# Two tile sizes that move SBUF addresses, and a new order for the first feed-forward step, in a two-layer hybrid decoder

## The chip, the cores and the metric

The kernel runs on one core of one Trainium2 chip. Time is the device time of one execution in microseconds. The span that a profile covers is shorter than that execution's own time by a little over 2 us here. Three runs of the kernel before lie within 0.1% of each other.

The engines are named as in the profile: PE is the TensorE matmul, PEld its load of the stationary operand, DVE VectorE, ACT ScalarE, POOL GpSimd, SP SyncE (here it issues the DMAs).

## The reference

A trunk of two layers on a sequence of 1024 rows of width 1024, in float32. Layer 0 mixes tokens with a gated linear recurrence, layer 1 with stick-breaking attention of 16 heads. Each mixer is followed by a feed-forward block of inner width 2816, and at the end there is a normalization.

```python
for layer in range(DEPTH):                      # DEPTH = 2
    hn = rms_norm(h, mix_norm[layer])
    mixed = rg_lru_block(hn, ...) if layer % 2 == 0 else stick_breaking_attention(hn, ...)
    h = h + mixed
    h = h + swiglu_ffn(rms_norm(h, ffn_norm[layer]), ffn_w_in[layer], ffn_w_out[layer])
return rms_norm(h, final_norm)

def swiglu_ffn(x, w_in, w_out):
    gu = x @ w_in
    return (silu(gu[..., :D_FF]) * gu[..., D_FF:]) @ w_out
```

## The kernel before

**Numbers.** Every float32 matmul is made of three in a reduced format (float32r): operand = high part + low part, and the product is high·high + low·high + high·low. The helper `mm3` (lines 639, 640 and 641) issues the three, each with 128x128 stationary and 128x512 moving operand, so almost every PE instruction of the page is one of these lines. ACT makes the high part (a copy that rounds), DVE the low part (a subtraction).

**Stages in time.** The recurrence and its projections run from 0 to about 321 us (the last 384 matmuls of it are its output projection), feed-forward 0 from there to about 965 us, attention to about 1470, attention's output projection to 1536, feed-forward 1 to the end.

**Feed-forward.** Both matrix products use Strassen-like schemes: a 2x2 block product is made from seven products (numbers 0 to 6, done in the order 0, 1, 2, 3, 4, 6, 5, `ORDER`). For the input side the seven combinations of the activations lie in SBUF once, as tiles `v[i, j]` (high `vh`, low `vl`; i is the product, j one of four blocks of the contraction). For each of the 22 column blocks f there is a *step* of 7 x 4 x 3 = 84 matmuls against seven combinations of that block's weights: `wa` serves products 0 and 1, `wb` 2 and 4, `wc` 3 and 5, `wd` 6 (with h or l for the part). The weights of a step are prepared during the step ahead of it by `a_hi`, `a_lo`, `s12`, `s2`, `s3`, `b_hi`, `do_s4`, and in the step itself by `b_lo`, `c_hi`, `c_lo`, `d_hi`, `d_lo` (lines 1116 to 1161). `post` takes a product out of its PSUM bank (lines 1302 to 1315), `gate` multiplies by the normalization factor and applies SiLU (1320 to 1326), and `operands` stores the result for the output side (1334 to 1350). The output side then runs 13 *visits* of the same seven products over 2 to 4 blocks each. Products that share a bank within a step (0, 2, 4, 5 in the first, 3 and 6 in the third, table `BANK`) accumulate on each other, so the next may start only when `post` has copied what was there.

**The first step.** The column block f = 0 is done ahead of the loop, all seven products at once in an order of its own (`P0`): first the blocks j = 0, 1, 2 of six products (54 matmuls), then j = 3 of the six and product 6. The first pass of the loop (`s_ == 0`, f = 1) also finishes the sums of squares of the normalization (`squares`), sums them over the partitions with PE (`Factors.sums`, line 597) and makes the factors (`all_factors`: two square roots and two squares on ACT, lines 600 and 603, four operations on DVE, lines 606 and 609), gates f = 0 and prepares f = 2. Its order is what the loop's body says. The order of the other engines in the loop is written out by hand too, as the body is emitted; in the recurrence and the attention a planner (`Plan`) sets it from estimated durations.

**Where tiles lie.** Pools are stacks. One grows from the low end of a partition's bytes: constants (`cp`), three raw weight buffers (`rp`), the activations `xh`/`xl` (`xp`), and later, in the place of these, part of the tiles `v` (`vp0`: all with i = 6, all with j = 3, and (5, 2)), the gate buffers, and the attention's pool `ap`. The other grows from the high end (`side="right"`): the ring of prepared weights (`wp`, `wq`), h, and the other tiles `v` (`vp1`). The last tile of `cp` is `minus` with 144 columns, of which only column 0 is used. In `ap` the tile `vt` holds 1024 columns and a margin of 32.

By the addresses of the build, the weight ring begins at byte 212864 of a partition and `vp1` at 85888; both leave 128 when divided by 256, and the tiles in them are multiples of 512 bytes. `minus` begins at 6592 and has 576 bytes, so `rp` begins at 7168 and `xp` and `vp0` at 19456, which leave 0. In `ap`, the two `vt` tiles (4224 bytes each) put about half of the tiles at 0 and half at 128.

Of the kernel before, what the change touches and what calls it, by code (L numbers as in the profile page):

```python
# [504 lines left out]
def trunk(  # L505
# [67 lines left out]
            for d in range(ND):  # L573
                x_[d] = [xp.tile([P, NB], F32R, name=f"{nm}{d}_{n}") for n in range(NH)]
    rcol = cp.tile([P, NT], F32, name="rcol")
    minus = cp.tile([P, 144], F32R, name="minus")
    fresh = tiny[:, 60:61]
    nc.gpsimd.memset(fresh, -(2.0**-41))
    nc.vector.tensor_copy(minus[:, 0:1], fresh)
# [31 lines left out]
    def all_factors(sums):  # L611
        for step in ("root", "square", "newton", "out"):
            for t in sums:
                getattr(t, step)()
# [444 lines left out]
    def mix_out_ffn_in(h, mix, bias, layer, gnext, ob):  # L1059
# [132 lines left out]
        with tc.manual_schedule(engines={E.PE, E.Activation, E.DVE, E.Pool}):  # L1192
# [505 lines left out]
            def seam(w):  # L1698
# [53 lines left out]
                pre["at"] = {k: end[t] - free["pe"] for k, t in marks.items()}  # L1752
                pre["raw"] = raws

            last_use = {p: max(u for u, (_, p0, p1) in enumerate(VISITS) if p0 <= p < p1) for p in range(NF // 2)}
            for s_, (kind, x) in enumerate(steps[:looped]):
                w, nw, ahead = nw, nxt, None
                if s_ + 2 < len(steps) - final:
                    ahead = weights_of(*steps[s_ + 2])

                g = {5: (0, 1), 6: (2, 3)} if s_ == 0 else {0: (1,), 1: (2,), 2: (3,)}
                gf = x - 1 if kind == "f" else NF - 1 if x == 2 else None
                if gf is not None and s_:
                    gate(gf, 0)
                if not w.ready:
                    w.b_lo()
                    if kind == "f":
                        w.c_hi()
                banks = {}
                if kind == "f":  # L1770
                    rhs = rhs_in
                else:
                    _, p0, p1 = VISITS[x]
                    rhs = {i: [R[p][i] for p in range(p0, p1)] for i in range(NPROD)}
                for k, i in enumerate(ORDER):
                    b = BANK[i]
                    new = b not in banks
                    if new:
                        banks[b] = pp.tile([P, NB], F32, tag="p", name=f"p{i}_ps")
                    if s_ == 0 and k == 4:  # L1780
                        part(banks[b], w, i, rhs[i], range(1), onto=not new)
                        for t in sums:
                            t.sums()
                        part(banks[b], w, i, rhs[i], range(1, HK), onto=not new)
                        UT.append(big("U", 2))
                        ta, tb = (pair_tile(x) for x in ("ta", "tb"))
                        nw.a_lo()
                        nw.s2()
                        nw.s3()
                        all_factors(sums)  # L1790
                    else:
                        part(banks[b], w, i, rhs[i], range(len(rhs[i])), onto=not new)
                    if kind == "f":
                        post(x, i, banks[b])
                    else:
                        old = done[:]
                        del done[:]
                        post_out(x, i, banks[b])
                        for dn in old:
                            if s_ == looped - 1 and k >= L - 2:  # L1800
                                done.append(dn)
                            else:
                                finished(*dn)
                    if s_ == 0:
                        if k < 2:
                            for _ in range(2):
                                squares(h, *sq_todo.pop(0), rbc, acc, V)

                    if k == 0:
                        if kind == "v":  # L1810
                            w.c_hi()
                        w.c_lo()
                    elif k == 2:
                        w.d_hi()
                        w.d_lo()
                        if nw:
                            nw.a_hi()
                        if s_ == 0:
                            for t in sums:
                                t.hi()  # L1820
                                t.lo()
                    elif nw:
                        if k == 3:
                            nw.s12()
                        elif k == 4 and s_:
                            nw.a_lo()
                            nw.s2()
                            nw.s3()
                        elif k == 5:
                            nw.b_hi()  # L1830
                            nw.do_s4()
                    if ahead and k == 3:
                        ahead.load_a()
                    elif ahead and k == 5:
                        ahead.load_b()

                    if gf is not None:
                        for y in g.get(k, ()):
                            gate(gf, y)
                        if gf % 2 == 0:  # L1840
                            if k == L - 1 and gf < NF - 2:
                                operands(gf // 2, 0)
                        elif 3 <= k <= 5:
                            if gf == NF - 1 and k == 3:
                                operands(gf // 2, 0)
                            operands(gf // 2, k - 2)

                    if kind == "f":
                        split_ahead(x - 7, k)
                    if kind == "f" and x == NF - 1:  # L1850
                        for p, y, _ in PLACES[k]:
                            if p < 2:
                                bring(p, y)
                        for y in {5: (0, 1, 2, 3, 4), 6: (6, 5)}.get(k, ()):
                            bring(2, y)
                    if kind == "v" and x == 0 and k == 5:
                        for y in ORDER:
                            bring(3, y)
                    if kind == "v":
                        gone = [p for p in range(NF // 2 - 4) if last_use[p] == x]  # L1860
                        for y, p in enumerate(gone):
                            bring(p + 4, i)
                            tasks.append((L * (x + 1) + k + 2 + y, p + 4, i))
                        if final and x == NV - 3 and k == 0:
                            for y in range(2):
                                bring(NF // 2 - 2 + y, 7, C[3][ORDER[y]])
                                tasks.append((L * (x + 1) + 3 + y, NF // 2 - 2 + y, 7))
                            d, p0, p1 = VISITS[NV - 1]
                            for y in range(2):
                                src = ffn_w_out[layer, d + y * HK][:, :, p0 * P : p1 * P]  # L1870
                                nc.sync.dma_start(held[5 + y].rearrange("p (y c) -> p y c", y=2), src)
                            nc.sync.dma_start(
                                held[3].rearrange("p (x c) -> p x c", x=2)[:, :, 0:P],
                                fin.broadcast_to([P, 2 * P]).rearrange("p (x c) -> p x c", x=2),
                            )
                            nc.scalar.sqrt(tiny[:, 62:63], ones)
                    if (kind == "v" and k < L - 1) or (kind == "f" and x == NF - 1):
                        now = k + (0 if kind == "f" else L * (x + 1))
                        tasks.sort(key=lambda t: t[0])
                        while tasks and tasks[0][0] <= now:  # L1880
                            split_op(*tasks.pop(0)[1:])
                nxt = ahead
                if kind == "v" and final:
                    if x == 2:
                        open_end()
                elif kind == "v":
                    if x == 2:
                        open_first()
                    elif x == NV - 3:
                        open_last()  # L1890
# [29 lines left out]
    with ExitStack() as st:  # L1920
# [51 lines left out]
        def scaled(q, which, n):  # L1972
            ps = PS.pop((q, which, n))
            if which < 2:
                t = TT[n] = own([P, NB], f"t{n}")
            else:
                if n == 0:
                    VT[q] = own([P, S + 32], f"vt{q % 2}")
                    nc.gpsimd.memset(VT[q][:, 15:16], 0.0)
                t = VT[q][:, 16 + n * NB : 16 + (n + 1) * NB]  # L1980
            V.tensor_mul(t, ps, rbc[n])
# [263 lines left out]
```

## Time and profile before

| | |
|---|---|
| median of 3 runs | 2198.35 us (2197.18 to 2198.82) |
| the profiled execution's own time | 2198.75 us |
| its span in the profile | 2196.5 us |
| PE, PEld busy | 2180.4 us (99%), 1782.3 us (81%) |
| DVE, ACT busy | 1714.3 us (78%), 1098.0 us (50%) |
| DMA | 274.61 MB, mean 125 GB/s |
| granted TensorE clock | 0.999 |

A PE row's duration (some 393 ns for 512 columns) is the time from the first column read to the last result and overlaps the next row's; what a matmul costs in a stream is the distance from its start to the start of the next. The rows of a timeline give starts to 0.01 us, so such a distance is best taken over many rows.

### The profile page before, as it was taken

What the parts mean: (1) busy time and instruction counts of PE and PEld (TensorE: products, weight loads), DVE (VectorE), ACT (ScalarE), POOL (GpSimd) and SP (SyncE); (2) the same over time, 40 slices, a digit from 0 to 9 for tenths busy, and PEclk for the clock granted to TensorE, in tenths of its full rate; (3) what the DMA queues carried; (4) which work ended last, traced back from release to release, by engine and by line L of the source; (5) the groups of instructions that cost most, each with busy time, mean ns of one, the idle gap of its engine ahead of it and who ended that gap; (6) DMA issues with size and microseconds to landing.
All of it is one profiled execution on the core that took longest, in us unless ns stands there. A gap on an engine that the chain in (4) does not pass through costs nothing.

```text
span 2196.5 us, 27019 instructions
## 1 busy us (share of the span) xinstructions
PE 2180.4 (99%) x9954; PEld 1782.3 (81%) x9954; DVE 1714.3 (78%) x2416; ACT 1098.0 (50%) x1793; POOL 29.3 (1%) x40
## 2 busy tenths in 40 slices
PE   9999999999999999999999999999999999999998
PEld 7888887888888888878888888888788888888887
DVE  8878678667777887888888888867866766777877
ACT  6577445344343544565555555544534434454555
POOL 0000020000000000000000000002000000000000
PEclk9999999999999999999999999999999999999999
DMA  4111312344443764444333333631133444467452
GB/s 174 39 48 48 119 45 68 105 129 145 144 149 128 258 213 125 141 135 113 92 101 93 100 92 101 186 143 65 58 115 117 144 143 143 140 224 245 129 160 84
DMA packets 133316, 274.61 MB, mean 125 GB/s; under 512 B 15296, under 2 KB 23872, under 8 KB 133184
## 3 DMA queue, kind: packets, MB, share of 16 engines
q1 hardware_dynamic: 132768, 272.36, 39.0%
q8 instruction: 78, 1.28, 0.2%
q10 hardware_dynamic: 416, 0.52, 0.1%
q14 instruction: 54, 0.44, 0.1%
HBM read 176.88 MB, written 70.78 MB: 113 GB/s over the span
## 4 chain that ended last, share of the span: by engine, by line
PE 97%; DVE 2%; ACT 1%; issue 0%; DMA 0%; DVEq 0%; ACTq 0%
PE p_ps L639 19%; PE p_ps L641 19%; PE p_ps L640 19%; PE qk_ps L639 4%; PE qk_ps L641 4%; PE qk_ps L640 4%; PE z_ps L2044 3%; PE av_ps L2092 3%; PE wt_ps L2075 3%; PE a_ps L640 3%; PE a_ps L641 3%; PE a_ps L639 3%; PE ob_ps L639 2%; PE ob_ps L640 2%; PE ob_ps L641 2%; PE g_ps L641 1%
## 5 line engine op out<-in xcount | busy, mean ns | idle before, releaser
L639 PE MATMUL p_ps<-vh,wbh 128*128 128x512 f32 x524 | 206.6, 394 | 3.3 <-ACT G L1302 2.2
L641 PE MATMUL p_ps<-vh,wbl 128*128 128x512 f32 x524 | 206.2, 394 | 3.2 <-DVE wbl L1142 3.2
L639 PE MATMUL p_ps<-vh,wch 128*128 128x512 f32 x524 | 206.1, 393 | 0.0
L641 PE MATMUL p_ps<-vh,wal 128*128 128x512 f32 x524 | 205.6, 392 | 0.2 <-DVE wal L1133 0.2
L640 PE MATMUL p_ps<-vl,wbh 128*128 128x512 f32 x524 | 205.8, 393 | 0.0
L640 PE MATMUL p_ps<-vl,wch 128*128 128x512 f32 x524 | 205.6, 392 | 0.0
L639 PE MATMUL p_ps<-vh,wah 128*128 128x512 f32 x524 | 205.6, 392 | 0.0
L641 PE MATMUL p_ps<-vh,wcl 128*128 128x512 f32 x524 | 205.4, 392 | 0.0
L640 PE MATMUL p_ps<-vl,wah 128*128 128x512 f32 x524 | 205.0, 391 | 0.0
L1138 ACT CAST wbh<-sb 128x1024 fp32r<-128x1024 f32 (+2 forms) x69 | 69.7, 1010 | 193.1 <-DVE sb L1122 193.1
L2056 ACT ACTIVATE F<-z_ps 128x512 f32<-128x512 f32 (+3 forms) x188 | 92.1, 490 | 98.3 <-PE z_ps L2044 97.1
L2080 ACT CAST th<-wt_ps 128x512 fp32r<-128x512 f32 x192 | 92.2, 481 | 85.1 <-PE wt_ps L2075 77.3
L2063 DVE TENSOR_TENSOR_SCAN F<-F,unit 128x128 f32<-128x128 f32 (+3 forms) x128 | 104.7, 820 | 33.6 <-ACT F L2056 32.5
L641 PEld LDWEIGHTS p_ps<-vh,wbl 128*128 128x128 f32 x524 | 98.6, 188 | 26.7 <-DVE wbl L1142 4.0
L639 PEld LDWEIGHTS p_ps<-vh,wbh 128*128 128x128 f32 x524 | 98.6, 188 | 26.4 <-ACT G L1302 3.0
L2084 DVE TENSOR_TENSOR tl<-wt_ps,th 128x512 fp32r<-128x512 f32 x192 | 104.6, 545 | 16.8 <-ACT th L2080 16.7
L641 PEld LDWEIGHTS p_ps<-vh,wal 128*128 128x128 f32 x524 | 98.3, 188 | 23.3 <-DVE wal L1133 1.3
L641 PEld LDWEIGHTS p_ps<-vh,wcl 128*128 128x128 f32 x524 | 98.3, 188 | 22.9 <-DVE wcl L1152 0.3
L640 PEld LDWEIGHTS p_ps<-vl,wch 128*128 128x128 f32 x524 | 98.5, 188 | 22.5
L640 PEld LDWEIGHTS p_ps<-vl,wbh 128*128 128x128 f32 x524 | 98.6, 188 | 22.2
L639 PEld LDWEIGHTS p_ps<-vh,wch 128*128 128x128 f32 x524 | 98.5, 188 | 22.2
L639 PEld LDWEIGHTS p_ps<-vh,wah 128*128 128x128 f32 x524 | 98.4, 188 | 22.2
(436 smaller groups left out, 5499.8 us busy)
## 6 DMA issues: line engine op xcount, KB each, us to landing
raw<-in_ffn_w_in SPq DMA_DIRECT2D x88, 512.0 KB, 3.6
vl<-pd SPq DMA_DIRECT2D x128, 256.0 KB, 3.4
pd<-U SPq DMA_DIRECT2D x90, 256.0 KB, 2.2
raw<-in_ffn_w_out SPq DMA_DIRECT2D x28, 512.0 KB, 4.0
raw<-in_attn_w_qkv SPq DMA_DIRECT2D x24, 512.0 KB, 3.8
kh<-qh SPq DMA_DIRECT2D x64, 128.0 KB, 2.3
kl<-ql SPq DMA_DIRECT2D x64, 128.0 KB, 2.3
acc<-pd SPq DMA_DIRECT2D x28, 256.0 KB, 2.6
```

The lines of the kernel that those rows point to most:

```text
L639: nc.tensor.matmul(ps, lhsT=wh, rhs=mh, start=first, stop=False, **kw)
L640: nc.tensor.matmul(ps, lhsT=wh, rhs=ml, start=False, stop=False, **kw)
L641: nc.tensor.matmul(ps, lhsT=wl, rhs=mh, start=False, stop=last, **kw)
L1138: nc.scalar.copy(self.full(self.wb), self.full(self.sb))
L2044: nc.tensor.matmul(ps[:, 0:n], lhsT=lhsT, rhs=rhs, start=i == 0, stop=i == 1)
L2056: nc.scalar.activation(F, Z.pop(c)[:, 0:n], AF.Sigmoid, scale=-SC)
L2063: V.tensor_tensor_scan(rev, rev, unit[:, NB - n :][:, ::-1], 0.0, op0=ALU.mult, op1=ALU.add)
L2075: nc.tensor.transpose(tp[:, c : c + P], F[:, (kb % 4) * P : (kb % 4 + 1) * P], ident)
L2080: nc.scalar.copy(WH[u][:, c:], TP[u][:, c:])
L2084: V.tensor_sub(WL[u][:, c:], TP.pop(u)[:, c:], f32(WH[u])[:, c:])
L2092: nc.tensor.matmul(ps[:, c:], lhsT=VV[q][:, kb, hx], rhs=t.pop(u)[:, c:], start=kb == 4 * G and i == 0, stop=kb == 3 and i == 1,)
```

## The change

Two tile sizes: `minus` shrinks from 144 to 112 columns (576 to 448 bytes), and `vt` grows from 1024 + 32 to 1024 + 64 columns (4224 to 4352 bytes). By the addresses of the new build, everything in the low stack behind `minus` moves down by 128 bytes: `rp` now begins at 7040, `xp` and `vp0` at 19328, and all 792 tiles of `ap` leave 128 when divided by 256. The high stack stays where it was. One pool that leaves 128 before leaves 0 now: `sp`, with the first four weight columns of the recurrence (`fh`, `fl`).

An order: in the first pass of each layer's loop, from product 2 on (k = 2 to 6), the body is replaced by a function `opening` that says what ACT, DVE and SP do after each product. It has the same instructions in another order; the `b_lo` of f = 2 is moved out of the second pass into the end of the first. PE's and SP's order is unchanged.

```diff
-    minus = cp.tile([P, 144], F32R, name="minus")
+    minus = cp.tile([P, 112], F32R, name="minus")
...
+            def opening(k, banks, w, nw, ahead):
+                ps = banks[BANK[ORDER[k]]]
+                if k == 2:
+                    post(1, 2, ps)
+                    for step in ("hi", "lo"):
+                        for t in sums:
+                            getattr(t, step)()
+                    w.d_hi()
+                    w.d_lo()
+                elif k == 3:
+                    nw.s12()
+                    nw.s2()
+                    nw.s3()
+                    ahead.load_a()
+                elif k == 4:
+                    all_factors(sums)
+                    post(1, 3, banks[BANK[3]])
+                    nw.a_hi()
+                    nw.a_lo()
+                    gate(0, 0)
+                    post(1, 4, ps)
+                    nw.b_hi()
+                elif k == 5:
+                    gate(0, 1)
+                    post(1, 6, ps)
+                    nw.do_s4()
+                    ahead.load_b()
+                else:
+                    post(1, 5, ps)
+                    nw.b_lo()
+                    gate(0, 2)
+                    gate(0, 3)
+                    operands(0, 0)
...
-                g = {5: (0, 1), 6: (2, 3)} if s_ == 0 else {0: (1,), 1: (2,), 2: (3,)}
+                g = {0: (1,), 1: (2,), 2: (3,)} if s_ else {}
...
                 if not w.ready:
-                    w.b_lo()
+                    if s_ != 1:
+                        w.b_lo()
                     if kind == "f":
                         w.c_hi()
...
-                        nw.a_lo()
-                        nw.s2()
-                        nw.s3()
-                        all_factors(sums)
                     else:
                         part(banks[b], w, i, rhs[i], range(len(rhs[i])), onto=not new)
+                    if s_ == 0 and k > 1:
+                        opening(k, banks, w, nw, ahead)
+                        continue
...
-                        if s_ == 0:
-                            for t in sums:
-                                t.hi()
-                                t.lo()
...
-                    VT[q] = own([P, S + 32], f"vt{q % 2}")
+                    VT[q] = own([P, S + 64], f"vt{q % 2}")
```

The order on ACT around the factors, in layer 0 (`U_2760` and `ta` hold the high parts of the sums of squares, `U_2548` is a gate buffer of f = 1, `p_ps` a product's bank, `wah` the weights of f = 2). Before:

```order
L1158 CAST wd<-s_2742 128x512
L1129 CAST wah<-raw 128x1024
L590 CAST U_2760<-acc_1874 128x512
L590 CAST ta<-acc_1875 128x512
L1308 COPY U_2548<-p_ps 128x512
L600 ACT_TABLE_LOAD
L600 ACTIVATE acc_1874<-ob,tiny 128x512
L600 ACTIVATE acc_1875<-ob,tiny 128x512
L603 ACTIVATE rbc_83<-acc_1874 128x512
L603 ACTIVATE rbc_84<-acc_1875 128x512
L1310 COPY U_2548<-p_ps 128x512
```

And now:

```order
L590 CAST U_2760<-acc_1874 128x512
L590 CAST ta<-acc_1875 128x512
L1158 CAST wd<-s_2742 128x512
L600 ACT_TABLE_LOAD
L600 ACTIVATE acc_1874<-ob,tiny 128x512
L600 ACTIVATE acc_1875<-ob,tiny 128x512
L603 ACTIVATE rbc_83<-acc_1874 128x512
L603 ACTIVATE rbc_84<-acc_1875 128x512
L1308 COPY U_2548<-p_ps 128x512
L1129 CAST wah<-raw 128x1024
L1310 COPY U_2548<-p_ps 128x512
```

The casts for the sums of squares come earlier, the copy of product 3 (L1308) now stands behind the four factor operations, and the weights `wah` stand behind it.

The order on DVE from the factors to the start of the second pass (`G_2545` and `U_2547` are f = 0's gate buffers, `G_2546` is f = 1's; `wbl` is f = 2's low part). Before:

```order
L609 SCALAR_TENSOR_TENSOR ob<-rbc_84,acc_1875 128x512
L1311 TENSOR_TENSOR U_2548<-U_2548 128x512
L1313 TENSOR_TENSOR G_2546<-G_2546,p_ps 128x512
L1125 TENSOR_TENSOR s_2868<-sb,raw 128x512
L1320 TENSOR_TENSOR G_2545<-ob,G_2545 128x1024
L1324 TENSOR_TENSOR G_2545<-ob,G_2545 128x1024
L1326 TENSOR_TENSOR U_2547<-U_2547,G_2545 128x1024
L1336 TENSOR_TENSOR ta<-U_2547 128x512
L1320 TENSOR_TENSOR G_2546<-ob,G_2546 128x1024
L1142 TENSOR_TENSOR wbl<-sb,wbh 128x1024
```

And now:

```order
L609 SCALAR_TENSOR_TENSOR ob<-rbc_84,acc_1875 128x512
L1133 TENSOR_TENSOR wal<-raw,wah 128x1024
L1320 TENSOR_TENSOR G_2545<-ob,G_2545 128x1024
L1311 TENSOR_TENSOR U_2548<-U_2548 128x512
L1313 TENSOR_TENSOR G_2546<-G_2546,p_ps 128x512
L1125 TENSOR_TENSOR s_2865<-sb,raw 128x512
L1142 TENSOR_TENSOR wbl<-sb,wbh 128x1024
L1324 TENSOR_TENSOR G_2545<-ob,G_2545 128x1024
L1326 TENSOR_TENSOR U_2547<-U_2547,G_2545 128x1024
L1336 TENSOR_TENSOR ta<-U_2547 128x512
L1320 TENSOR_TENSOR G_2546<-ob,G_2546 128x1024
```

The low part `wbl` (L1142) moves ahead of f = 0's second and third gate operations and of f = 1's first; `wal` (L1133) moves from before the factors to behind them. Layer 1 has the same two changes.

More of the change, by code (lines that the diff above doesn't have):

```diff
@@ L1804, in mix_out_ffn_in @@
                     if s_ == 0:
-                        if k < 2:
-                            for _ in range(2):
-                                squares(h, *sq_todo.pop(0), rbc, acc, V)
+                        for _ in range(2):
+                            squares(h, *sq_todo.pop(0), rbc, acc, V)
                     if k == 0:
@@ L1824, in mix_out_ffn_in @@
                             nw.s12()
-                        elif k == 4 and s_:
+                        elif k == 4:
                             nw.a_lo()
```

## The prediction

> **What bounds the kernel now.** I read the page's busy shares and the chain of waits first, then PE's waits, then PE's timeline, since the first two leave only one engine.
>
> ```profile
> PE 2180.4 (99%) x9954; PEld 1782.3 (81%) x9954; DVE 1714.3 (78%) x2416; ACT 1098.0 (50%) x1793; POOL 29.3 (1%) x40
> PE 97%; DVE 2%; ACT 1%; issue 0%; DMA 0%; DVEq 0%; ACTq 0%
> PE p_ps L641 <- DVE wbl L1142: 3.2, 2, 1.6
> PE p_ps L639 <- ACT G L1302: 2.2, 2, 1.1
> PE a_ps L774 <- POOL ident masks.py:199: 1.5, 1, 1.5
> PE p_ps L639 <- ACT ta L1738: 1.2, 1, 1.2
> ```
>
> The last four rows are PE's longest waits of the whole execution: total, times, longest. Two of the four are the two layers' openings, 5.4 us together. Nothing else is on the path but the stream of matmuls itself. So the question is how fast that stream runs, and whether it runs equally fast everywhere. It doesn't:
>
> ```profile
> 322.87 0.39 PE L639 MATMUL p_ps<-vh,wah 128*128 128x512 f32 x1
> ...
> 332.39 0.40 PE L639 MATMUL p_ps<-vh,wch 128*128 128x512 f32 x1
> ...
> 340.08 0.39 PE L639 MATMUL p_ps<-vh,wah 128*128 128x512 f32 x1
> ```
>
> This is the column block done ahead of the loop in layer 0. From 320.81 to 332.39 PE runs 51 matmuls whose `v` tiles lie in the high stack (blocks 0 to 2 of six products, without (5, 2)); all operands leave 128 modulo 256. From its tenth on (322.87) these are 42 in 9.52 us, 226.7 ns each. From 332.39 to 340.08 come 33 whose `v` tiles lie in the low stack and leave 0, against weights that leave 128: 7.69 us, 233.0 ns each. Same instruction, same weights' ring, no wait in either, 6.3 ns apart.
>
> Now the same distance where the kernel spends its time:
>
> ```profile
> 52.01 0.40 PE L639 MATMUL a_ps<-xh,whi 128*128 128x512 f32 x1
> ...
> 320.81 0.39 PE L639 MATMUL p_ps<-vh,wah 128*128 128x512 f32 x1
> 480.11 0.39 PE L639 MATMUL p_ps<-vh,wah 128*128 128x512 f32 x1
> ...
> 499.47 0.39 PE L639 MATMUL p_ps<-vh,wah 128*128 128x512 f32 x1
> 978.63 0.39 PE L639 MATMUL qk_ps<-xg,whi 128*128 128x512 f32 x1
> ...
> 993.96 0.23 PE L2044 MATMUL z_ps<-kh,q 128*128 128x128 f32 x1
> 1469.55 0.39 PE L639 MATMUL ob_ps<-vh,whi 128*128 128x512 f32 x1
> ...
> 1536.47 0.39 PE L639 MATMUL p_ps<-vh,wah 128*128 128x512 f32 x1
> ```
>
> Recurrence and its output projection: 1152 matmuls from 52.01 to 320.81, all with moving operands in the low stack, 268.80 / 1152 = 233.3 ns. One feed-forward step: 84 in 19.36 us = 230.5 ns; 33 of its 84 read low-stack tiles. Attention's projections where nothing is between them: 66 in 15.33 us = 232.3 ns. Attention's output projection in layer 1: 288 in 66.92 us = 232.4 ns. Every stretch falls between the two values of the pair above, the feed-forward step, where most addresses agree, lowest.
>
> **The change part by part.** *Addresses.* The new sizes put both operands at 128 modulo 256 everywhere but in the first 192 matmuls. I take 226.7 ns for each matmul of 512 columns and subtract:
> - recurrence: 1152 x (233.3 - 226.7) = 7.6 us;
> - feed-forward: 22 steps x 84 + 44 blocks x 21 = 2772 in a layer, 5544 in all, x (230.5 - 226.7) = 21.1 us;
> - output projection of layer 1: 288 x (232.4 - 226.7) = 1.6 us;
> - attention: 1152 projection matmuls x (232.3 - 226.7) = 6.4 us. The products z and av have 384 more of 512 columns, mixed with 128-wide ones; no row there is a clean pair, so they are worth 0 to 2.2 us.
>
> What hides behind PE must keep up:
>
> ```profile
> 50.00:308.00 258.00, 258.00 (x1108) 207.51 (x1107) 198.13 (x232) 148.26 (x170) 9.07 (x7) 1.00 0.19 60
> 400.00:900.00 500.00, 500.00 (x2171) 407.01 (x2170) 372.36 (x519) 219.03 (x346) 0.00 (x0) 1.00 0.48 158
> 980.00:1477.00 497.00, 496.15 (x2633) 414.92 (x2632) 418.03 (x619) 270.72 (x539) 0.59 (x6) 1.00 0.39 111
> ```
>
> After the length come PE, PEld, DVE, ACT. DVE is busy 77%, 74% and 84% of these stretches, so a PE that is 1.6 to 2.8% faster doesn't reach it on average. In the attention the chain z, sigmoid, scan, transpose, av goes round all engines with two banks each, and local waits can eat a part; its bounds are 0 (DVE paces it) and 8.6 us, and I take 5.5, nearer the upper, because PE waits nowhere in its main part. Sum of the addresses: 7.6 + 21.1 + 1.6 + 5.5 = 35.8 us.
>
> *The openings.* Layer 0, second pass, product 2:
>
> ```profile
> 365.96 0.40 PE L641 MATMUL p_ps<-vh,wal 128*128 128x512 f32 x1
> 367.44 0.50 PE L639 MATMUL p_ps<-vh,wbh 128*128 128x512 f32 x1 [1.08 <-ACT G L1302]
> 367.78 0.39 PE L640 MATMUL p_ps<-vl,wbh 128*128 128x512 f32 x1
> 369.76 0.50 PE L641 MATMUL p_ps<-vh,wbl 128*128 128x512 f32 x1 [1.59 <-DVE wbl L1142]
> 360.46 0.39 PE L641 MATMUL p_ps<-vh,wcl 128*128 128x512 f32 x1
> 365.49 1.23 DVE L1326 TENSOR_TENSOR U<-U,G 128x1024 f32<-128x1024 f32 x1
> 366.80 0.59 ACT L1302 COPY G<-p_ps 128x512 f32<-128x512 f32 x1 [1.09 <-DVE U L1326]
> 368.49 1.22 DVE L1142 TENSOR_TENSOR wbl<-sb,wbh 128x1024 fp32r<-128x1024 f32 x1
> ```
>
> Starts that should be 0.23 us apart are 1.48 and 1.98 apart: 1.25 + 1.75 = 3.0 us lost a layer. Cause: the copy L1302 of product 0 into f = 0's buffer waits for the last gate operation (L1326) on that buffer, and `wbl` stands behind it on DVE. Now `wbl` comes first. Its ring buffer is `wch` of the pass before, free when that pass's last product ends (360.46 in the old order), so it runs from about 361.5 to 362.7; L1324 and L1326 follow, 1.23 us each, to 365.2; the copy ends near 365.9. PE wants bank and weights at 366.7, later by the new stall below. Both waits go, with under a microsecond to spare.
>
> Something is late in their place: product 6 accumulates onto product 3's bank, and the copy L1308 of that bank now stands behind the factors.
>
> ```profile
> 348.32 0.39 PE L641 MATMUL p_ps<-vh,wbl 128*128 128x512 f32 x1
> 348.75 0.59 ACT L1306 COPY G<-p_ps 128x512 f32<-128x512 f32 x1 [0.83 <-PE p_ps L641]
> 352.72 0.48 PE L597 MATMUL ob<-tb,minus 128*128 128x512 f32 x1
> 353.64 1.27 ACT L600 ACTIVATE acc<-ob,tiny 128x512 f32<-128x512 f32 x2
> 354.80 1.16 ACT L603 ACTIVATE rbc<-acc 128x512 f32<-128x512 f32 x2
> 355.85 0.58 ACT L1310 COPY U<-p_ps 128x512 f32<-128x512 f32 x1
> 355.12 0.39 PE L639 MATMUL p_ps<-vh,wd 128*128 128x512 f32 x1
> ```
>
> ACT follows a PE result 0.43 us after that matmul's start (348.32 to 348.75). The square roots need the sums, last started at 352.72, so they begin near 353.15 instead of 353.64 (the table load before them is earlier by the copy that left, and no longer the last to finish). L603 comes 1.16 later, L1308 another 1.05 later, at 355.36, and ends 0.59 later at 355.95. Product 6 would start at 355.12. New stall: about 0.9 us a layer; bounds 0.4 (if the square roots take the first sum as soon as it is there) and 1.2. Net 3.0 - 0.9 = 2.1 a layer, 4.2 us.
>
> *The clock.* In layer 1 the same two stalls end in a stretch at a lower clock:
>
> ```profile
> 1586.00:1590.00 4.00, 4.00 (x12) 3.13 (x11) 2.30 (x3) 0.58 (x2) 0.00 (x0) 0.57 0.43 131
> ```
>
> The granted clock was 0.57 in these 4 us, 4 x 0.43 = 1.7 us lost; layer 0, with equal stalls, has no such stretch. With one stall of 0.9 us in place of two within 4 us I take the 1.7 back. [...]
>
> *Nothing else.* The order of PE and SP is the same, so no transfer is issued earlier or later by the order; `vt`'s extra columns aren't touched.
>
> Sum: 35.8 + 4.2 + 1.7 = 41.7 us from the profiled execution's 2198.75 gives 2157.0; the median lies 0.4 below that execution, so 2156.7. I say **2157 us**.
>
> **The rivals.** *Other engines pace the attention and the output visits.* For it: DVE's 84%. Against it: no PE wait in the attention's main part. Then 5.5 us and 44 x 21 x 2 x 3.8 ns = 7.0 us stay: about 2169.5.
>
> *The addresses are not the cause.* The pair differs also in which block is done; were it the tile's place in the scheme, only the openings would count: 2198.35 - 5.9 = 2192.5. Against it: the recurrence has no scheme, all its moving tiles in the low stack, and 233.3 ns.
>
> [...]
>
> *Slower: agreement is what costs.* Operands at the same place in a 256-byte line could collide at every read, and the weight load become the bound.
>
> ```profile
> L639 PEld LDWEIGHTS p_ps<-vh,wbh 128*128 128x128 f32 x524 | 98.6, 188 | 26.4 <-ACT G L1302 3.0 <-ACT ta L1738 1.6
> ```
>
> A load takes 188 ns and fits under a matmul with some 40 to spare. If it grew past 233, each nanosecond over would cost 8.1 us on the 8,136 matmuls named above (mean now 231.2); at 237 ns it would be 2198 + 47 - 6 = 2239. It decides from 232 ns on, where the openings' 5.9 us are used up. Against it: 51 matmuls in agreement at 320.81 to 332.39 show the opposite.
>
> *The change doesn't do what it says*: a pool's start could be rounded up again. The build's addresses speak against that; 2192.5 again.
>
> **How the numbers follow.** Forecast 72%, other engines pace 16%, addresses not the cause or not moved 7%, agreement costs 3%, the rest 2%. The forecast's own bounds: attention 0 to 8.6 us, openings' stall 0.4 to 1.2 in two layers, the clock 0 to 1.7, and small new waits of about 2 us: 2152 to 2167. For 8 in 10 I reach to the second case and a little past both: 2148 to 2171. Less than 0.2% (4.4 us) can't be told from no change here. Faster 95%, same 2%, slower 3%.
>
> **What would show it.** In the recurrence the 1152 matmuls should take 261.2 us (226.7 each), a step of feed-forward 19.04 us, the projections of the attention 15.0 us for 66. If they stay at 233.3, 230.5 and 232.3, the addresses fall. PE's list of waits should lose `wbl` and L1302 and gain the copy L1308 at two times about 0.9 us, and the clock row of layer 1 should read 1.00. If the attention stays at its length while its PE gains waits on DVE, the second case holds. I am wrong above 2171 or below 2148.

## The result, and the profile after

The changed kernel takes **2163.56 us** (median of 4 runs, 2163.40 to 2163.97); the kernel before takes 2198.41 beside it. The ratio is 0.9843, with a 95% interval of 0.9826 to 0.986: 34.9 us less, where 41.7 were forecast. The profiled execution took 2163.40 us with a span of 2161.1.

First the page's shares, busy time by engine and the chain that ended last.

```profile
PE 2148.0 (99%) x9954; PEld 1781.1 (82%) x9954; DVE 1716.3 (79%) x2416; ACT 1098.5 (51%) x1793; POOL 29.2 (1%) x40
PE 96%; DVE 2%; ACT 2%; issue 0%; DMA 0%; SPq 0%; DVEq 0%; ACTq 0%
```

The start of PE's list of waits (total us, times, longest):

```profile
PE p_ps L639 <- ACT U L1308: 1.6, 2, 0.8
PE a_ps L774 <- POOL ident masks.py:199: 1.5, 1, 1.5
PE p_ps L639 <- ACT ta L1738: 1.2, 1, 1.2
```

The waits on `wbl` and L1302 are gone, and the copy L1308 is there twice with 0.8. PE still bounds the kernel, as before: the time came out of the stream of matmuls itself. PE's timeline at the ends of the stretches (start, duration, operation):

```profile
51.89 0.39 PE L639 MATMUL a_ps<-xh,whi 128*128 128x512 f32 x1
...
313.02 0.39 PE L639 MATMUL p_ps<-vh,wah 128*128 128x512 f32 x1
...
371.68 0.39 PE L641 MATMUL p_ps<-vh,wcl 128*128 128x512 f32 x1
...
390.72 0.39 PE L641 MATMUL p_ps<-vh,wcl 128*128 128x512 f32 x1
...
946.14 0.39 PE L639 MATMUL qk_ps<-xg,whi 128*128 128x512 f32 x1
...
959.30 0.39 PE L639 MATMUL qk_ps<-xg,whi 128*128 128x512 f32 x1
...
974.29 0.22 PE L2073 MATMUL z_ps<-kh,q 128*128 128x128 f32 x1
...
1448.98 0.39 PE L639 MATMUL ob_ps<-vh,whi 128*128 128x512 f32 x1
...
1514.28 0.39 PE L639 MATMUL p_ps<-vh,wah 128*128 128x512 f32 x1
```

Recurrence and projection: 313.02 - 51.89 = 261.13 us for 1152 matmuls, 226.7 ns each (before 268.80). One step of feed-forward: 19.04 us for 84 (19.36). The 66 undisturbed projections of the attention: 14.99 us (15.33). The output projection of layer 1: 65.30 us for 288 (66.92). All four are what was forecast.

The attention is the exception. From its first projection to its output projection it takes 1448.98 - 946.14 = 502.84 us. Before, the row of its start, beside the end at 1469.55 that the prediction quotes, is

```profile
965.44 0.40 PE L639 MATMUL qk_ps<-xg,whi 128*128 128x512 f32 x1
```

so it was 504.11 us. The gain is 1.27 us, where the sum held 5.5, and no wait on DVE or ACT in the list has grown to account for it. (A row lasts 0.39 us and the next starts 0.23 us later, so a delay under some 0.16 us doesn't show there; only the starts do.) The terms, forecast and measured between the same starts in both traces:

| term | forecast us | measured us |
|---|---|---|
| recurrence and projection | 7.6 | 7.7 |
| feed-forward, both layers, with openings and clock | 21.1 + 4.2 + 1.7 = 27.0 | 11.5 + 13.3 = 24.8 |
| output projection, layer 1 | 1.6 | 1.6 |
| attention | 5.5 | 1.3 |
| sum | 41.7 | 35.4 |

The profiled executions differ by 2198.75 - 2163.40 = 35.35.

The new opening in layer 0, PE, ACT and DVE:

```profile
346.76 0.39 PE L641 MATMUL p_ps<-vh,wbl 128*128 128x512 f32 x1
347.33 0.58 ACT L1308 COPY U<-p_ps 128x512 f32<-128x512 f32 x1
347.96 0.50 PE L639 MATMUL p_ps<-vh,wd 128*128 128x512 f32 x1 [0.82 <-ACT U L1308]
353.69 1.22 DVE L1142 TENSOR_TENSOR wbl<-sb,wbh 128x1024 fp32r<-128x1024 f32 x1
```

Product 6 waits for the copy, 0.82 us, and `wbl` is computed long before PE wants it. And a window of layer 1 around the same place (length, busy times of PE, PEld, DVE, ACT and POOL, granted clock, DMA share, GB/s):

```profile
1546.00:1566.00 20.00, 19.18 (x85) 15.55 (x84) 18.28 (x23) 13.12 (x20) 0.00 (x0) 1.00 0.23 79
```

The granted clock is 1.00 there.

### The profile page after: what moved, and what is told of

It reads as the page before. It is cut to its first block, busy times and chain, and to the rows that moved or that the text cites. A ratio compares the mean times of both kernels' runs of the same rounds, so it can differ in the third digit from the quotient of the medians.

```text
span 2161.1 us, 27023 instructions
## 1 busy us (share of the span) xinstructions
PE 2148.0 (99%) x9954; PEld 1781.1 (82%) x9954; DVE 1716.3 (79%) x2416; ACT 1098.5 (51%) x1793; POOL 29.2 (1%) x40
## 4 chain that ended last, share of the span: by engine, by line
PE 96%; DVE 2%; ACT 2%; issue 0%; DMA 0%; SPq 0%; DVEq 0%; ACTq 0%
PE p_ps L641 18%; PE p_ps L639 18%; PE p_ps L640 18%; PE qk_ps L639 4%; PE qk_ps L641 4%; PE qk_ps L640 4%; PE z_ps L2073 3%; PE av_ps L2121 3%; PE wt_ps L2104 3%; PE a_ps L640 3%; PE a_ps L641 3%; PE a_ps L639 3%; PE ob_ps L639 2%; PE ob_ps L640 2%; PE ob_ps L641 2%; PE g_ps L640 1%
## 5 line engine op out<-in xcount | busy, mean ns | idle before, releaser
L640 PEld LDWEIGHTS p_ps<-vl,wah 128*128 128x128 f32 x524 | 98.4, 188 | 20.5
```

What stands on the lines that cost most here:

```text
L640: nc.tensor.matmul(ps, lhsT=wh, rhs=ml, start=False, stop=False, **kw)
```

## The experiments

**Sizes alone, order alone.** The kernel before with

```
-    minus = cp.tile([P, 144], F32R, name="minus")
+    minus = cp.tile([P, 112], F32R, name="minus")
-                    VT[q] = own([P, S + 32], f"vt{q % 2}")
+                    VT[q] = own([P, S + 64], f"vt{q % 2}")
```

> The order of before, with the two new sizes (112 columns of minus, 64 spare columns of v). Theory (addresses and openings are two separate gains): of the 34.9 us measured, 29.0 are the addresses, so 2198.4 - 29.0 = 2169.4 us, with the recurrence's 1152 matmuls in 261.1 us, and the waits on wbl and L1302 still in the list (3.0 us a layer). If the low clock of layer 1 doesn't come with them, 1.7 less: 2167.7. Rival (the addresses are not the cause): 2198.4, the recurrence at 268.8.

Measured: 2172.67 us, ratio 0.9877 (0.9862 to 0.9892); the recurrence took 261.16. The addresses are the cause of the recurrence's gain, but the whole is 3.3 us slower than I expected. Rows of PE's timeline, and then of windows in both layers:

```profile
359.65 0.50 PE L639 MATMUL p_ps<-vh,wbh 128*128 128x512 f32 x1 [1.30 <-ACT G L1302]
361.97 0.51 PE L641 MATMUL p_ps<-vh,wbl 128*128 128x512 f32 x1 [1.59 <-DVE wbl L1142]
```

```profile
363.00:367.00 4.00, 4.00 (x12) 3.11 (x12) 1.85 (x3) 1.05 (x3) 0.00 (x0) 0.60 0.48 131
1565.00:1571.00 6.00, 4.33 (x11) 3.17 (x12) 5.28 (x7) 1.09 (x2) 0.00 (x0) 0.73 0.44 159
```

The two old stalls are still there, and this time a stretch at a low clock stands behind them in both layers (0.60 and 0.73 in these windows), not in layer 1 alone. So the openings are worth more beside the new sizes: 2172.67 - 2163.56 = 9.1 us, not 5.9. The granted clock varies from one execution to the next: it was 0.997 in all four executions of sizes alone, but 0.996 (2203.37 us) to 0.999 (2197.24 us) in the eight of the kernel before beside them. The slowed starts here run from 362.78 to 366.14 (3.36 us) and from 1567.73 to 1571.14 (3.41 us). What decides whether a pair of stalls is followed by such a stretch isn't shown: in the trace of the kernel before it came in layer 1, and with equal stalls not in layer 0. Nor is it shown that the faster rate is what brings both stretches.

The reverse, the changed kernel with 144 and `S + 32`:

> The new order with the two old sizes. Theory: only the openings' gain, 2198.4 - 5.9 = 2192.5 us; the recurrence stays at 268.8 us, the feed-forward step at 19.36 us, the waits on wbl and L1302 are gone and one of about 0.9 us a layer on the copy of product 3 is there. Rival (the order is the cause of most): 2163.6. Rival (the openings' gain exists only at the faster matmul rate): 2198.

Measured: 2191.82 us, 0.9965 (0.9952 to 0.9978); recurrence 268.80, the two old waits gone, L1308 there with 1.6 us in two waits. Between the traces the order brings 2.28 us in layer 0's feed-forward and 3.89 in layer 1's, 6.2 together: the forecast's openings and clock, 5.9, were right at the old rate. Sizes alone bring 25.7 us (2198.41 - 2172.67) and order alone 6.6; the remaining 2.5 of the 34.9 come only with both. Against the kernel before that ran beside these two (2199.01) they bring 26.3 and 7.2, which leaves 1.4, so this remainder is known only roughly.

**Which address counts.** The changed kernel, with the moving operands left at 0 modulo 256 and the weights moved to 0 as well:

```
-    minus = cp.tile([P, 112], F32R, name="minus")
+    minus = cp.tile([P, 144], F32R, name="minus")
-    edge.tile([P, 24], F32, name="edge")
+    edge.tile([P, 56], F32, name="edge")
```

> The new order and the wider v tile, but the low stack left at 0 modulo 256 (144 columns of minus) and the high stack moved down by 128 bytes, so that moving operands and weights lie at 0 modulo 256 together. Theory (agreement counts, not where it is): as after, 2163.6 us, within 1 us; recurrence 261.1 us. Rival (a moving operand has to lie at 128 modulo 256, or away from the start of a 256-byte line): 2192.5 us, recurrence 268.8 us.

Measured: 2164.03 us, recurrence 261.12. Agreement counts, not the place. Then the low stack 64 bytes off (`minus` of 128 columns), and 256 bytes off (176 columns):

> After, with minus 16 columns wider, so that the low stack lies 64 bytes from the weights modulo 256 in place of 0. Theory (every disagreement modulo 256 costs): the recurrence at 268.8 us (233.3 ns each), the whole near 2192.5 us. Rival (only half a line, 128 bytes, costs, or agreement modulo 64 is enough): 261.1 us and 2163.6.

> After, with minus 64 columns wider: the low stack lies 256 bytes further, so operands agree modulo 256 and no longer modulo 512. Theory (256 is the length that counts): recurrence 261.1 us, the whole 2163.6 within 1 us. Rival (512 counts): between 228.9 and 233.3 ns in the recurrence, the whole 2185 to 2192.

```profile
52.17 0.40 PE L639 MATMUL a_ps<-xh,whi 128*128 128x512 f32 x1
...
315.86 0.39 PE L639 MATMUL p_ps<-vh,wah 128*128 128x512 f32 x1
```

256 bytes off: 2163.49 us (one run) and 261.16 in the recurrence, so agreement modulo 256 is enough. 64 bytes off, shown here: 2188.49 us (one run). In the recurrence 263.69 / 1152 = 228.9 ns, between the two known values, so neither expectation held there; in layer 0's feed-forward 643.40 us, as long as with 128 bytes off (642.35 in the order alone). 64 bytes of disagreement cost too, but not by a rule that these runs show.

Why 64 bytes cost as much as 128 in feed-forward shows in part inside a step, where blocks that agree and blocks that don't take turns. From the step of the kernel before that the prediction quotes, three disagreeing matmuls of product 0, nine agreeing ones of product 1, then disagreeing ones again:

```profile
484.92 0.40 PE L639 MATMUL p_ps<-vh,wah 128*128 128x512 f32 x1
...
485.62 0.39 PE L639 MATMUL p_ps<-vh,wbh 128*128 128x512 f32 x1
...
487.68 0.40 PE L639 MATMUL p_ps<-vh,wbh 128*128 128x512 f32 x1
```

The nine agreeing intervals are 230 236 229 232 231 227 226 227 227 ns: behind the disagreeing ones the rate comes back only step by step. Over 14 steps of the order alone the 51 agreeing matmuls average 229.4 ns and the 12 of product 6, all disagreeing, 233.1. With 64 bytes off the 51 average 231.6 and the 12 only 229.1. So there the agreeing neighbours pay most of the price; why they pay more at 64 bytes stays open.

**The attention: who paces it?** The rival of the prediction was DVE. But PE's list of waits gained nothing there, so the starts must tell. Behind product 6's stall, where nothing but 512-wide matmuls follow, the changed kernel shows

```profile
348.30 0.39 PE L640 MATMUL p_ps<-vl,wd 128*128 128x512 f32 x1
...
349.69 0.39 PE L640 MATMUL p_ps<-vl,wd 128*128 128x512 f32 x1
...
351.96 0.39 PE L641 MATMUL p_ps<-vh,wcl 128*128 128x512 f32 x1
```

The first 6 intervals take 1.39 us, 232 ns each (231 231 235 229 232 231 one by one), the next 10 take 2.27, 227 each. Agreeing operands bring 226.7 ns only after a few matmuls in a row: six intervals here, nine or ten behind the other waits of layer 0's feed-forward (from 738.00: 229 234 236 224 231 235 229 232 231, then 227). And this is the attention:

```profile
1101.86 0.49 PE L2104 MATMUL wt_ps<-ident,F 128*128 128x128 f32 x3
1102.10 0.48 PE L639 MATMUL qk_ps<-vh,whi 128*128 128x512 f32 x1
1102.42 0.39 PE L640 MATMUL qk_ps<-vl,whi 128*128 128x512 f32 x1
...
1104.26 0.39 PE L641 MATMUL qk_ps<-vh,wlo 128*128 128x512 f32 x1
1104.49 0.38 PE L2104 MATMUL wt_ps<-ident,F 128*128 128x128 f32 x2
```

Ten wide matmuls stand between narrow transposes here. The attention has 200 groups of transposes, and on the diagonal the products z and av have under 512 columns too, so most runs are shorter: 179 of three matmuls of 512 columns, 89 of five, 44 of ten. From 1102.42 to 1104.26 are 8 intervals in 1.84 us, 230 ns; behind the group before (from 1099.78) they are 229 233 236 224 231 236 228 233, nearly the sequence behind the wait in feed-forward, where only wide matmuls follow. New theory: each narrow group starts the settling anew, and most runs of the attention end before it is over. To test it where no other engine is near its limit, I cut matmuls in the recurrence into narrow ones, with both pairs of sizes. This is the body of the helper that the recurrence calls in place of `mm3`:

```
+        turns[0] += 1
+        if turns[0] % 3:
+            mm3(ps, wh, wl, mh, ml, first, last)
+            return
+        nc.tensor.matmul(ps, lhsT=wh, rhs=mh, start=first, stop=False)
+        for i in range(4):
+            c = slice(i * P, (i + 1) * P)
+            nc.tensor.matmul(ps[:, c], lhsT=wh, rhs=ml[:, c], start=False, stop=False, skip_group_check=True)
+        nc.tensor.matmul(ps, lhsT=wl, rhs=mh, start=False, stop=last)
```

> After, but in the recurrence (864 matmuls, before the output projection) one in nine is issued as four of 128 columns, with the same weights and into the same sums, so that runs of eight wide matmuls stand between narrow ones, as in the attention. Theory (settling: after a group of narrow matmuls it takes about ten wide ones, at 231 to 236 ns each, before agreeing addresses give 226.7): wide to wide intervals in the recurrence rise to a mean of 231 to 232 ns, while the projection behind it, without cuts, stays at 226.7. Rival (another engine paces the attention, and wide matmuls run at 226.7 whatever stands between them): 226.7 in both.

> The same cuts with the two old sizes. Both theories: wide to wide intervals of 233 ns in the recurrence and in the projection. Theory (settling): the recurrence's 864 matmuls take only 0.5 to 2 us longer than with the new sizes (768 wide ones by 1 to 2 ns). Rival: 768 by 6.6 ns, 5.1 us longer.

(The recurrence has 768 of the 1152 matmuls, not 864; 85 were cut. Each kernel with cuts ran once.) New sizes, start of the recurrence, one run between two cuts, start and end of the projection:

```profile
52.48 0.40 PE L639 MATMUL a_ps<-xh,whi 128*128 128x512 f32 x1
...
150.70 0.56 PE L653 MATMUL a_ps<-xl,whi 128*128 128x128 f32 x4
151.10 0.44 PE L654 MATMUL a_ps<-xh,wlo 128*128 128x512 f32 x1
151.38 0.40 PE L639 MATMUL a_ps<-xh,whi 128*128 128x512 f32 x1
...
152.77 0.40 PE L650 MATMUL a_ps<-xh,whi 128*128 128x512 f32 x1
153.00 0.56 PE L653 MATMUL a_ps<-xl,whi 128*128 128x128 f32 x4
...
248.67 0.39 PE L639 MATMUL ob_ps<-xh,whi 128*128 128x512 f32 x1
...
335.74 0.39 PE L639 MATMUL p_ps<-vh,wah 128*128 128x512 f32 x1
```

and with the old sizes:

```profile
51.99 0.40 PE L639 MATMUL a_ps<-xh,whi 128*128 128x512 f32 x1
...
248.20 0.40 PE L639 MATMUL ob_ps<-xh,whi 128*128 128x512 f32 x1
...
337.80 0.39 PE L639 MATMUL p_ps<-vh,wah 128*128 128x512 f32 x1
```

With cuts the recurrence takes 196.19 us with agreeing addresses and 196.21 with disagreeing ones: the gain is gone to the last 0.02 us, where the theory had left 0.5 to 2. The projection right behind it has no cuts and keeps its gain, 87.07 against 89.60. Within a run from 151.38 to 152.77, 6 intervals average 232 ns. Over the recurrence the intervals behind another wide matmul average 231.4 ns, and 232.5 with the old sizes, where 233 was expected; the narrow groups and the interval behind each take that last difference back. The rival, with 226.7 between the cuts, falls.

Then in the attention itself. In 184 of the 192 groups of the weights' tiles, 544 of 576 transposes are left out, with two matmuls as wide as the group in their place (the expectation's 368 is the number of these matmuls):

```
+            if q in VV:
+                c, v = begin(u), VV[q].rearrange("p t h c -> p (t h c)")
+                for i in range(2):
+                    nc.tensor.matmul(tp[:, c:], lhsT=v[:, 0:P], rhs=v[:, c:NB], start=i == 0, stop=i == 1)
+                return
```

> After, but in the attention 368 of the 400 transposes of the weights' tiles are left out; two matmuls as wide as the group, on tiles of v, write the bank in place of each group of four. What follows works on those values. Theory (settling): with the narrow groups gone, intervals between wide matmuls in the attention come to 227 to 229 ns, except behind the products on the diagonal, which stay narrow. Rival (another engine paces the attention): they stay at 230 to 231 and PE gains waits.

> The same with the two old sizes. Theory (settling): the attention from its first projection to its last is 3 to 5 us longer than with the new sizes, where with transposes it was 1.3 longer. Rival: 1.3 as before.

New sizes, then old:

```profile
946.41 0.39 PE L639 MATMUL qk_ps<-xg,whi 128*128 128x512 f32 x1
...
1453.59 0.40 PE L639 MATMUL ob_ps<-vh,whi 128*128 128x512 f32 x1
```

```profile
962.24 0.40 PE L639 MATMUL qk_ps<-xg,whi 128*128 128x512 f32 x1
...
1473.30 0.40 PE L639 MATMUL ob_ps<-vh,whi 128*128 128x512 f32 x1
```

507.18 against 511.06 us: the sizes now differ by 3.9 us in the attention, with transposes by 1.3. Intervals behind another wide matmul average 229.2 ns, just above the 227 to 229 expected, against 232.0. The matmuls put in don't wait for the scans as the transposes did, so this pair alone wouldn't exclude DVE. But PE's lists of waits show no wait on a scan with or without the transposes, and the cuts in the recurrence removed the gain with every other dependence in place. So the narrow groups kept the gain away, not another engine.

**Fewer interruptions.** The changed kernel, with two groups of transposes side by side where the plan allows it:

```
-        T[u] = plan.add("pe", 0.109 * len(js) + 0.02, fn["T", u, len(ring)], need, u - 1.8)
+        T[u] = plan.add("pe", 0.109 * len(js) + 0.02, fn["T", u, len(ring)], need, u // 2 * 2 - 1.8)
```

> After, with the rank of every second group of transposes in the attention's plan lowered by one unit, so that two groups stand together: 124 groups of transposes in place of 200, and runs of 20 wide matmuls in place of 10. Theory (settling): each group costs the wide matmuls behind it about 43 ns (the intervals 235 233 236 224 231 236 228 233 230 less 226.7 each), so 76 x 43 ns = 3.3 us less: 2160.3 us. Rival (other engines pace the attention): PE gains waits on the scans and on th and tl, and the time is 2163.6 or longer.

Measured: 2162.87 us (2162.50 to 2163.56), 0.7 less than after, not 3.3. That is hardly more than the 0.4 by which the kernel before differed between the two sets of runs; the attention's 501.73 us, 1.1 less, is clearer, since it was 502.84 both after and in the run with cuts. No wait grew by more than 0.1 us. The price per group was set too high; the likely reason is that the narrow products z and av on the diagonal stay where they were and start the settling too. Of the wide intervals behind another wide one, 980 averaged 230.3 ns with single groups, and 1128 average 229.5 in pairs. The direction fits the theory; the size doesn't.

**A better version.** Two edits to the changed kernel, the copy of product 3 ahead of the factors, and the first 192 matmuls' weights moved to agreement:

```
+        sp.tile([P, 32], F32, name="gap")
-                    all_factors(sums)
                     post(1, 3, banks[BANK[3]])
+                    all_factors(sums)
```

> After, with two more edits: the copy L1308 of product 3 stands ahead of the factors in the opening, and the pool of the first 192 matmuls' weights begins 128 bytes later, so that they agree as well. Theory: the opening's stall of 0.87 us a layer goes (1.7 us) and 192 matmuls of 233.5 ns take 226.7 (1.3 us): 2160.6 us. Rival for the first (the stall only moves: the square roots start 0.4 to 0.6 us later and a later copy is late): 2162.3. Rival for the second (the first matmuls are paced by the loads and casts): 2161.9. Both rivals: 2163.6.

Measured: 2172.90 us, 9.3 slower than after. One row from its list of waits, then two from the timelines of PE and DVE:

```profile
PE g_ps L640 <- DVE rl L968: 6.1, 1, 6.1
```

```profile
51.23 0.39 PE L641 MATMUL a_ps<-xh,fl 128*128 128x512 f32 x1
51.66 0.17 DVE L912 COPY u<-nbias 128x3 f32<-128x3 f32 x1 [9.97 <-PE a_ps L641]
```

The pool of the recurrence takes over the first pool's bytes. Shifted by 128, the last of the weights `fl` ends 128 bytes inside `u`, and DVE waits 9.97 us with `u` for the last matmul that reads `fl`. Between 40.04 and 65.05 us of the changed kernel's time 9.6 us were lost; the openings' part brought 0.5 us a layer (1.1 gained at product 6, 0.6 lost behind it, where the copy L1302 is late). The next version moves the recurrence's pool too, gives the copy to DVE, and keeps the pairs of transposes as above:

```
+        sp.tile([P, 32], F32, name="gap")
+        lp.tile([P, 64], F32, name="gap2")
                 elif k == 3:
+                    V.tensor_copy(halves(1)[3], ps)
-                    post(1, 3, banks[BANK[3]])
```

> After with three edits: the pairs of transposes of the run before (0.7 us); the copy of product 3 given to DVE, right behind product 3 (removes 0.87 us a layer, 1.7 in all, without the 0.4 us that the square roots were late in the run with the copy ahead on ACT); the pool of the first weights 128 bytes later and the recurrence's pool 256 bytes later, so that u no longer lies on the last of the first weights (0.7 to 1.3 us, and none of the 8.9 us lost there). Theory: 2163.6 - 0.7 - 1.7 - 1.0 = 2160.2 us. Rival for the opening (the copy L1302 is late in place of it): 2161.3. Rival for the pool (another pair of tiles shares bytes): 2165 to 2169.

Measured: **2160.08 us** (2159.45 to 2161.03), ratio to before 0.9824 (0.981 to 0.9837), 3.5 less than after and 3.4 less than the kernel 256 bytes off beside it. The profiled execution was the slowest of the five (2161.03), and the spans are 2.4 apart (2161.1 and 2158.7): 0.8 before the recurrence, 1.7 in the two openings, with no wait of product 6 left in the list, and 0.35 in the attention, where the rest of the pairs' gain goes with a new wait of 0.8 us of the transposes on DVE; about 0.5 goes back in layer 1's feed-forward, which I didn't trace further. So the median met the sum of 2160.2, but the trace accounts for 2.4 of the 3.4 us forecast: the attention's part fell short, and that the median agrees to 0.1 us is in part luck.

## Why the prediction was right, and where its sum was off

- *PE's stream is the bound, and the addresses set its rate*: right, and shown by sizes alone and by the mirror. 226.7 ns held in the recurrence, the step and the output projection to 0.1 ns.
- *The pair of column blocks as evidence*: right. It was a clean comparison because nothing interrupts either part; that it was uninterrupted was a condition I didn't see. It stood in the rows: the prediction counts from the tenth matmul on without saying why, and the first three intervals, behind disagreeing matmuls, are 232, 233 and 230 ns. The recurrence's 233.3 also lies just above the pair's 233.0, not between its two values.
- *Attention, 5.5 us within 0 to 8.6*: the term that was mis-sized; it measured 1.3. The prediction took the 232.3 ns of 66 matmuls in a row for all 1152, and took the upper half "because PE waits nowhere". The question it put was which other engine might pace the attention. None did: in the runs with cuts (231.4 ns against 232.5 with the old sizes) and without transposes (229.2 against 232.0) it is the interruption of PE's own stream that keeps the rate from settling. The 981 wide intervals behind another wide one went from 232.0 only to 230.3 ns; at 226.7 they would have brought 981 x (232.0 - 226.7) = 5.2 us.
- *Feed-forward, 21.1 us*: measured 24.8 - 6.2 = 18.6. The step's gain is exact; the loss lies in places where the stream is interrupted or agreed already, such as the seam into the attention (layer 0's last 88 matmuls took 21.67 us before, with most intervals at 226 to 231 ns already, and 21.76 after) and the output visits with short waits. That these waits cost more than their length by new settling was seen at a few of them, not tested alone.
- *Openings, 4.2 us, and the clock, 1.7*: right beside the old sizes (6.2 for both). The new stall was put at 0.9 and is 0.82 as a wait, 1.0 from start to start. What the prediction didn't see is that its one low stretch was that of one execution: with sizes alone both layers had one in the traced execution, and the kernel before ran at a granted clock of 0.996 to 0.999. Whether the faster stream itself makes such stretches more frequent isn't shown.
- *The second case* (other engines pace attention and output visits, 2169.5) gave the attention's length nearly right for a wrong reason; the prediction's own test for it, PE gaining waits on DVE, failed. *Addresses not the cause* and *agreement costs* are excluded.

Open: why agreeing operands need up to ten matmuls to settle, and what 64 bytes do. Other distances weren't tried.

## What to carry to other kernels

Measure the distance from one matmul's start to the next, by stretch: if PE is never idle and the distance differs between like stretches, look at the addresses of both operands. Scale such a gain only over matmuls that stand in runs as long as the one it was measured in; here four narrow ones after every eight wide ones took all of it (5.1 us), and behind three whose operands disagree the first five agreeing ones took 229 to 236 ns in place of 226.7. Padding also moves what shares bytes with what: after a shift of 128 bytes, look for tiles that begin under the end of another one (DVE waited 9.97 us for such a one here).

## What the hardware showed that I had not expected

- A matmul of 512 columns that loads new weights each time started every 226.7 ns where moving operand and weights agreed modulo 256 bytes, every 233.3 ns at 128 bytes apart in the recurrence (232.4 in layer 1's output projection, 66.92 us for 288), and every 228.9 ns at 64 bytes in the recurrence, though in layer 0's feed-forward 64 bytes cost as much as 128 (643.40 us against 642.35).
- The fast rate is a state that is reached: after an interruption three to ten intervals of 224 to 240 ns come first. Four narrow matmuls after every eight wide ones removed the whole difference of 5.1 us (174.08 against 179.20 uncut, 196.19 against 196.21 cut).
- Behind two stalls of 1.3 and 1.6 us within 4 us the starts were 0.43 us apart in place of 0.227 for 3.4 us, in both layers of the traced execution of sizes alone; behind stalls of 1.1 and 1.6 us in the kernel before they were so in one layer of two.
